# Moving small tiles in SBUF so that moving operands and weights lie a multiple of 256 bytes apart, in a two-layer trunk of SwiGLU, SSD and S5

## The chip, the cores and the metric

The kernel runs on one core of one Trainium2 chip. The metric is the device time of one execution in microseconds (us); times below one microsecond are in nanoseconds (ns). Times come from timed runs and from one execution recorded by the hardware profiler.

## The reference

The input is `x` of 512 tokens by 1024 channels in float32. Two layers follow each other, and each is a half-weighted SwiGLU, a token mixer, and another half-weighted SwiGLU. The mixer of the first layer is a Mamba-2 SSD, that of the second an S5 diagonal state space model.

```python
def swiglu(h, w_in, w_out):                      # w_in 1024 x 5632, w_out 2816 x 1024
    gate, up = jnp.split(h @ w_in, 2, axis=-1)
    return (jax.nn.silu(gate) * up) @ w_out

for i in range(2):
    x = x + 0.5 * swiglu(rmsnorm(x, ffn1_norm[i]), ffn1_w_in[i], ffn1_w_out[i])
    h = rmsnorm(x, mix_norm[i])
    x = x + (ssd_mixer(h, ...) if i == 0 else s5_mixer(h, ...))
    x = x + 0.5 * swiglu(rmsnorm(x, ffn2_norm[i]), ffn2_w_in[i], ffn2_w_out[i])
return rmsnorm(x, final_norm)
```

The SSD mixer projects to 6176 columns, convolves over time, scans in chunks over 32 heads with a state of 128, gates, normalises and projects 2048 channels back to 1024. The S5 mixer scans 64 groups of 16 channels with a complex state of 64, applies a GELU and a gated projection of 1024 to 2 x 1024.

## The kernel before

Activations lie transposed: channels on the 128 partitions, 512 tokens along the free dimension. `xT` is the residual stream, eight tiles of 128 x 512. Matrix products keep nearly all of float32's precision: each operand is split into a high part, rounded to TensorE's faster float32 format, and the low rest, and three products are added into one PSUM bank. `proj` does this for one output tile of 128 channels, over `n` slices of 128 input channels:

```python
for k in range(n):
    PE.matmul(ps, hi[:, k], H[k], start=first and k == 0, stop=False)             # L276
    PE.matmul(ps, hi[:, k], L[k], start=False, stop=False)                        # L277
    PE.matmul(ps, lo[:, k], H[k], start=False, stop=last and k == n - 1)          # L278
```

The second argument is the weights (128 x 128, 512 bytes of a partition), the third the moving operand (128 x 512, 2048 bytes of a partition). Weights arrive by DMA in `wst`; ScalarE rounds them into `whi` (L267), VectorE writes the rest into `wlo` (L269). The moving operands have names by stage:

- `hH`, `hL`: the normalised input of an FFN or of the SSD mixer (pool `hpool`). In the S5 mixer the same tiles hold some of its gate weights.
- `ah`, `al`: the product of gate and up inside an FFN, moving operand of its out projection (pool `ffn`, on the right side of SBUF).
- `yh`, `yl`: the SSD mixer's output, moving operand of its out projection (pool `ssd`).
- `gh`, `gl`: the S5 mixer's GELU output, moving operand of its gated projection (pool `s5`).
- `hx`, `hy`: sums for the second layer's in projections, which use a Winograd form with seven products of 256 columns in place of eight (`Seven`, L361). Two of its weight tiles, `wh22` and `wl22`, come from the pool `ffn`. `Seven.prod` adds one of the seven products:

```python
for j in range(KD // 2):
    bh, bl = self.pr.B[bn, j]
    for w_, b_ in ((hi, bh), (hi, bl), (lo, bh)):
        PE.matmul(ps, w_[:, j], b_, start=nm not in self.open, stop=False, skip_group_check=True)   # L361
```

An FFN's hidden width of 2816 is worked in three parts of 8, 7 and 7 slices of 128. For each part all in projections of the part run first (moving operand `hH`, `hL`), then eight out projections, one for each of the eight `xT` tiles (moving operand `ah`, `al`), so a stretch of in projections and a stretch of 8 x 3 x 7 = 168 or 8 x 3 x 8 = 192 matmuls of out projections take turns:

```python
pd = mm_ps()
proj(pd, load_w(w_out[a * 128:b * 128, d * 128:(d + 1) * 128], b - a), AH, AL)
V.scalar_tensor_tensor(xT[d], pd, 0.5, xT[d], op0=OP.mult, op1=OP.add)      # L596
```

SBUF is handed out as two stacks. The left one grows from 16,512 bytes of each partition upward: first the pool `const`, then `wpool` (`wst`, `whi`, `wlo`), `hpool`, `work`, and above them the pools of the stages. The right one grows downward from the end and holds a filler of 24 numbers and, inside an FFN, the pool `ffn`. So whatever `const` takes moves every later tile of the left stack and none of the right one. `small` (L49 to L51) hands out small tiles, padded to 32 numbers, that is 128 bytes. In `const`, `small` makes `kmask` and `qres` (L71, L72, selection masks for the S5 mixer), `cols0` to `cols3` (L96, columns of gains and biases, read by `col`) and `warm` (L106, one column used only at the start). In the SSD mixer it makes `acol`, `cse`, `dce` and the two `raw` tiles, which lie below `yh` and `yl` in their stack.

The order of work is written out by hand for TensorE (`manual_schedule`); for the other engines a scheduler sets it when the program is built. Weights are loaded by SP's queue ahead of use, through four `wst`, three `whi` and three `wlo` buffers.

Of the kernel before, what the change touches and what calls it, by code (L numbers as in the profile page):

```python
# [9 lines left out]
F32 = mybir.dt.float32  # L10
# [21 lines left out]
def trunk_kernel(ctx, tc, x, ffn1_norm, ffn1_w_in, ffn1_w_out, mix_norm, ffn2_norm, ffn2_w_in, ffn2_w_out,  # L32
# [4 lines left out]
    V, S, G, PE = nc.vector, nc.scalar, nc.gpsimd, nc.tensor  # L37

    const = ctx.enter_context(tc.tile_pool(name="const", bufs=1))
    const.tile([128, 64], F32, name="fill_left")  # L40
    right = ctx.enter_context(tc.tile_pool(name="right", bufs=1, side="right"))
    right.tile([128, 24], F32, name="fill_right")
    wpool = ctx.enter_context(tc.tile_pool(name="wpool", bufs=3))
# [4 lines left out]

    def small(pool, p, n, name, **kw):  # L49

        return pool.tile([p, -(-n // 32) * 32], F32, name=name, **kw)[:, :n]  # L51

    def mm_ps():
        return psum.tile([128, 512], F32, tag="mm", name="mm", bufs=4)
# [1 line left out]
    def aux_ps():  # L56
        return psum.tile([128, 512], F32, tag="aux", name="aux", bufs=4)
# [5 lines left out]
    def rows_ap(src, r0, n, w=128):  # L63
        return bass.AP(tensor=src.tensor, offset=src.offset + r0 * w, ap=[[w, n], [1, w]])
# [3 lines left out]
    make_identity(nc, ident)  # L68
    ones = const.tile([128, 128], F32, name="ones")
    V.memset(ones, 1.0)  # L70
    kmask = small(const, 128, 16, "kmask")  # L71
    qres = small(const, 128, 8, "qres")  # L72
    qsel = const.tile([128, 128], F32, name="qsel")

    def masks():
# [17 lines left out]


    vrow = [xin.tile([n, 128], F32, name=f"vrow{i}") for i, n in enumerate((104, 128, 18, 16))]
    cols = [small(const, 128, v.shape[0], f"cols{i}") for i, v in enumerate(vrow)]  # L96
    C = {"f1": (3, 0), "cw": (1, 0), "sd": (2, 0), "dtb": (2, 16), "al": (2, 17)}

    def cols_of(i):
# [3 lines left out]
        V.tensor_copy(cols[i], p[:, :n])  # L103

    tc.keep_in_program_order(nc.scalar.dma_start(vrow[3], rows_ap(ffn1_norm, 0, 16)))
    warm = small(const, 128, 1, "warm")  # L106
    r = 0
    for nm, src, n in (("mix", mix_norm, 16), ("f2", ffn2_norm, 16), ("fin", final_norm, 8),
                       ("gn", ssd_gate_norm, 16), ("cb", ssd_conv_b, 32), ("gb", s5_glu_b, 16)):
# [1367 lines left out]
    with tc.manual_schedule(engines={mybir.EngineType.Activation, mybir.EngineType.DVE, mybir.EngineType.PE}):  # L1477
# [23 lines left out]
        p = aux_ps()  # L1501
# [114 lines left out]
```

## Time and profile before

| | |
|---|---|
| median of three timed runs | 2073.85 us (2071.47 to 2077.07) |
| profiled execution, its own time | 2071.94 us |
| profiled execution, span from first to last instruction | 2070.2 us |
| mean granted TensorE clock | 0.989 of full speed |
| TensorE busy | 2028.3 us, 98% of the span |
| VectorE, ScalarE, GpSimd busy | 1410.9, 849.9 and 95.2 us |
| matmuls of the split format with 512 columns | 7128 |
| matmuls of the split format with 256 columns | 2016 |

In rows of the profile PE is a matmul on TensorE and PEld a weight load, which runs beside the matmuls; DVE is VectorE, ACT ScalarE, POOL GpSimd, SP SyncE. `mm<-hH,whi` reads: writes the PSUM tile `mm` from the moving tile `hH` and the weights `whi`. A group's row ends with the count, the busy time in us with the mean in ns, and the idle time ahead of it with what ended it. A row of the timeline begins with start and duration in us. The row of an operation's durations has its least, its median and its greatest in ns.

### The profile page before, as it was taken

The numbers are of one execution on the slowest core, as the hardware profiler recorded it, in microseconds if no ns is written. First come the engines' busy times: TensorE is split into PE (matmuls) and PEld (weight loads), VectorE is DVE, ScalarE is ACT, GpSimd is POOL, SyncE is SP. The second block draws the span as 40 slices with busy tenths as digits, with TensorE's granted clock in tenths as the row PEclk, the third lists the DMA queues.
The fourth block names the chain that finished last, engine by engine and source line by source line (L and its number), as shares of the span: only waits on it lengthen the run. The fifth ranks groups of instructions, "written<-read, shape, count | busy, mean of one in ns | idle before, by whom it ended". The sixth has DMA issues, their size and how long they took to land.

```text
span 2070.2 us, 29322 instructions
## 1 busy us (share of the span) xinstructions
PE 2028.3 (98%) x11555; PEld 1704.8 (82%) x11555; DVE 1410.9 (68%) x2390; ACT 849.9 (41%) x1394; POOL 95.2 (5%) x148
## 2 busy tenths in 40 slices
PE   9999999999999999999999999999996999999997
PEld 7888888888878887877778888898885889888896
DVE  6889445688875887568854776574768577556574
ACT  5223233556653564333422443242454444233343
POOL 1000000021110110000000000000011000000000
PEclk9999999999999999999999999999997999999999
DMA  6354542343333324435553223323387123333341
GB/s 183 99 157 160 150 112 84 109 123 99 120 118 92 105 74 147 131 117 157 151 160 96 88 82 113 92 80 107 108 277 244 51 70 114 102 92 94 91 119 55
DMA packets 411529, 244.42 MB, mean 118 GB/s; under 512 B 44952, under 2 KB 396864, under 8 KB 411136
## 3 DMA queue, kind: packets, MB, share of 16 engines
q1 hardware_dynamic: 381968, 203.19, 34.1%
q0 software_dynamic: 7984, 25.46, 3.7%
q10 hardware_dynamic: 21440, 13.91, 2.2%
q8 instruction: 90, 1.47, 0.3%
q14 instruction: 47, 0.39, 0.1%
HBM read 217.74 MB, written 24.25 MB: 117 GB/s over the span
## 4 chain that ended last, share of the span: by engine, by line
PE 91%; DVE 5%; ACT 2%; issue 1%; DMA 0%; SPq 0%; DVEq 0%; ACTq 0%
PE mm L276 25%; PE mm L277 25%; PE mm L278 25%; PE mm L361 12%; PE aux L836 1%; DVE cv L697 1%; DVE wlo L269 0%; PE aux L778 0%; PE aux L1349 0%; PE aux L741 0%; PE aux L829 0%; DVE z L1331 0%; PE aux L278 0%; PE aux L277 0%; PE aux L276 0%
## 5 line engine op out<-in xcount | busy, mean ns | idle before, releaser
L276 PE MATMUL mm<-hH,whi 128*128 128x512 f32 x1416 | 558.1, 394 | 0.6 <-DVE gt L570 0.6
L277 PE MATMUL mm<-hL,whi 128*128 128x512 f32 x1416 | 553.4, 391 | 0.0
L278 PE MATMUL mm<-hH,wlo 128*128 128x512 f32 x1416 | 552.8, 390 | 0.0
L267 ACT CAST whi<-wst 128x1024 fp32r<-128x1024 f32 (+2 forms) x269 | 267.6, 998 | 585.9 <-PE mm L277 443.8
L269 DVE TENSOR_TENSOR wlo<-wst,whi 128x1024 fp32r<-128x1024 f32 (+2 forms) x269 | 310.6, 1157 | 34.6 <-ACT whi L267 32.3
L278 PEld LDWEIGHTS mm<-hH,wlo 128*128 128x128 f32 x1416 | 266.0, 188 | 57.2 <-DVE wlo L269 0.6
L276 PEld LDWEIGHTS mm<-hH,whi 128*128 128x128 f32 x1416 | 266.2, 188 | 56.6 <-issue 2.7
L277 PEld LDWEIGHTS mm<-hL,whi 128*128 128x128 f32 x1416 | 266.3, 188 | 53.0 <-issue 0.6
L277 PE MATMUL mm<-al,whi 128*128 128x512 f32 x704 | 278.3, 395 | 0.0
L278 PE MATMUL mm<-ah,wlo 128*128 128x512 f32 x704 | 278.2, 396 | 0.0
L276 PE MATMUL mm<-ah,whi 128*128 128x512 f32 x704 | 277.8, 396 | 0.0
L596 DVE SCALAR_TENSOR_TENSOR xT<-mm,xT 128x512 f32<-128x512 f32 x96 | 66.0, 689 | 161.1 <-PE mm L278 160.8
L277 PEld LDWEIGHTS mm<-al,whi 128*128 128x128 f32 x704 | 132.4, 188 | 31.4 <-issue 0.6
L278 PEld LDWEIGHTS mm<-ah,wlo 128*128 128x128 f32 x704 | 132.4, 188 | 31.3 <-issue 0.2
L276 PEld LDWEIGHTS mm<-ah,whi 128*128 128x128 f32 x704 | 132.4, 188 | 31.0 <-issue 0.4
L305 DVE TENSOR_TENSOR wlo<-wst,whi 128x1024 fp32r<-128x1024 f32 x88 | 107.6, 1223 | 26.3 <-ACT whi L300 26.3
L300 ACT CAST whi<-wst 128x512 fp32r<-128x512 f32 x176 | 100.3, 621 | 21.8 <-PE mm L277 18.1
L573 DVE TENSOR_TENSOR up<-mm,rbc 128x512 f32<-128x512 f32 x44 | 30.3, 689 | 83.8 <-PE mm L278 83.5
L697 DVE SCALAR_TENSOR_TENSOR cv<-raw,cols,cv 128x512 f32<-128x512 f32 x96 | 81.0, 850 | 7.6 <-ACT cv L695 6.7
L361 PE MATMUL mm<-hH,whi 128*128 128x256 f32 x288 | 82.5, 286 | 0.3 <-ACT up L378 0.2
L361 PE MATMUL mm<-hH,wlo 128*128 128x256 f32 x288 | 82.0, 285 | 0.0
L361 PE MATMUL mm<-hL,whi 128*128 128x256 f32 x288 | 82.0, 285 | 0.0
(395 smaller groups left out, 2897.0 us busy)
## 6 DMA issues: line engine op xcount, KB each, us to landing
wst<-in_ffn_w_in_dram SPq DMA_DIRECT2D x176, 512.0 KB, 3.9
wst<-in_ffn_w_out_dram SPq DMA_DIRECT2D x64, 448.0 KB, 3.6
wst<-in_ssd_in_proj_dram SPq DMA_DIRECT2D x48, 512.0 KB, 3.8
wst<-in_ffn_w_out_dram SPq DMA_DIRECT2D x32, 512.0 KB, 3.6
dec<-d_cs POOLq DMA_DIRECT2D x16, 512.0 KB, 4.3
opP<-d_P SPq DMA_DIRECT2D x16, 512.0 KB, 6.5
wst<-in_s_glu_w_dram POOLq DMA_DIRECT2D x12, 512.0 KB, 5.1
d_t<-p_cs POOLq DMA_DIRECT2D x8, 512.0 KB, 4.4
```

The source lines that it names most:

```text
L267: S.copy(hi, st)
L269: V.tensor_tensor(lo, st, hi.bitcast(F32), op=OP.subtract)
L276: PE.matmul(ps, hi[:, k], H[k], start=first and k == 0, stop=False)
L277: PE.matmul(ps, hi[:, k], L[k], start=False, stop=False)
L278: PE.matmul(ps, lo[:, k], H[k], start=False, stop=last and k == n - 1)
L300: self.pin(S.copy(hi[:, hs[i]], st[i] if type(st) is list else st[:, hs[i]]))
L305: self.pin(V.tensor_tensor(lo[:, b], a, hi[:, b].bitcast(F32), op=OP.subtract))
L361: PE.matmul(ps, w_[:, j], b_, start=nm not in self.open, stop=False, skip_group_check=True)
L573: V.tensor_tensor(up, pu, pr.rbc, op=OP.mult)
L596: V.scalar_tensor_tensor(xT[d], pd, 0.5, xT[d], op0=OP.mult, op1=OP.add)
L697: V.scalar_tensor_tensor(cv, raw[:, 1 + j:T + 1 + j], col("cw", j * 32 + ct), cv, op0=OP.mult, op1=OP.add)
L836: PE.matmul(py[hh * 64:(hh + 1) * 64, s], st["dtx"][:, c, k0:k0 + 64], M[:, hh, s], start=True, stop=True)
```

## The change

A filler at the bottom of `const` goes, `small` pads to 64 numbers (256 bytes) in place of 32, and five small tiles of `const` (`kmask`, `qres`, `cols2`, `cols3`, `warm`) become slices of one tile `few` of 64 numbers.

```diff
     const = ctx.enter_context(tc.tile_pool(name="const", bufs=1))
-    const.tile([128, 64], F32, name="fill_left")
...
     def small(pool, p, n, name, **kw):
-        return pool.tile([p, -(-n // 32) * 32], F32, name=name, **kw)[:, :n]
+        return pool.tile([p, -(-n // 64) * 64], F32, name=name, **kw)[:, :n]
...
-    kmask = small(const, 128, 16, "kmask")
-    qres = small(const, 128, 8, "qres")
+    few = const.tile([128, 64], F32, name="few")
+    kmask = few[:, 0:16]
+    qres = few[:, 16:24]
...
-    cols = [small(const, 128, v.shape[0], f"cols{i}") for i, v in enumerate(vrow)]
+    cols = [small(const, 128, v.shape[0], f"cols{i}") for i, v in enumerate(vrow[:2])] + [few[:, 26:44], few[:, 44:60]]
...
-    warm = small(const, 128, 1, "warm")
+    warm = few[:, 24:25]
```

In both programs each engine's instructions stand in the same order and with the same shapes; after the change ScalarE has one more wait on semaphores, for DMAs of GpSimd's queue in the first FFN. The starts of the tiles move: `const` shrinks by 640 bytes (256 + 5 x 128 go, 256 come), and everything above it on the left stack sinks by as much, but for `yh` and `yl`, below which five small tiles of the SSD mixer grow by 128 bytes each. This is where the tiles of the wide matmuls begin in a partition, by the places that the two programs give them (a tile with several buffers by its first; its other buffers are multiples of 512 bytes further):

| tile | start before | modulo 256 | start after | modulo 256 |
|---|---|---|---|---|
| `whi`, `wlo` (weights) | 53,248 and 65,536 | 0 | 52,608 and 64,896 | 128 |
| `hH`, `hL` | 77,824 and 94,208 | 0 | 77,184 and 93,568 | 128 |
| `hy`, `hx` | 121,344 and 129,536 | 0 | 120,704 and 128,896 | 128 |
| `gh`, `gl` | 193,536 and 209,920 | 0 | 192,896 and 209,280 | 128 |
| `yh`, `yl` | 188,032 and 204,416 | 128 | 188,032 and 204,416 | 128 |
| `ah`, `al` | 196,480 and 212,864 | 128 | 196,480 and 212,864 | 128 |
| `wh22`, `wl22` (weights) | 188,288 and 190,336 | 128 | 188,288 and 190,336 | 128 |

Slices of these tiles begin at further multiples of 512 bytes, so the last columns hold for every wide matmul. Before, 2496 matmuls of 512 columns (those of `ah`, `al`, `yh`, `yl`) and 288 of 256 columns (those of `wh22`, `wl22`) have a moving operand 128 bytes off a multiple of 256 from their weights; after, none has. Tiles that other engines use moved too: `wst` begins at 36,864 (0 modulo 256) before and at 36,224 (128) after, the sums in `rbc` and `sq` likewise from 0 to 128, while `xT`, `cv` and `y` are at 128 before and after.

## The prediction, made before the changed kernel ran

> **What bounds the kernel now.** I read the page's busy times first, then the chain that ended last, then the groups of instructions.
>
> ```profile
> span 2070.2 us, 29322 instructions
> PE 2028.3 (98%) x11555; PEld 1704.8 (82%) x11555; DVE 1410.9 (68%) x2390; ACT 849.9 (41%) x1394; POOL 95.2 (5%) x148
> PE 91%; DVE 5%; ACT 2%; issue 1%; DMA 0%; SPq 0%; DVEq 0%; ACTq 0%
> L276 PE MATMUL mm<-hH,whi 128*128 128x512 f32 x1416 | 558.1, 394 | 0.6 <-DVE gt L570 0.6
> L277 PE MATMUL mm<-hL,whi 128*128 128x512 f32 x1416 | 553.4, 391 | 0.0
> L278 PE MATMUL mm<-hH,wlo 128*128 128x512 f32 x1416 | 552.8, 390 | 0.0
> L277 PE MATMUL mm<-al,whi 128*128 128x512 f32 x704 | 278.3, 395 | 0.0
> L278 PE MATMUL mm<-ah,wlo 128*128 128x512 f32 x704 | 278.2, 396 | 0.0
> L276 PE MATMUL mm<-ah,whi 128*128 128x512 f32 x704 | 277.8, 396 | 0.0
> L276 PE MATMUL mm<-yh,whi 128*128 128x512 f32 x128 | 51.9, 405 | 0.3 <-ACT yh L855 0.3
> ```
>
> TensorE is the bound: 98% of the span, 91% of the chain, and almost no idle time ahead of any wide group. So what one matmul costs is what counts. The last column but one is the duration of a record, whose end is modelled and which overlaps the next; it hints at a few ns between hH and ah, but it isn't a price. The price is the distance from one start to the next, so I took stretches of the timeline in which nothing else runs on TensorE. Each pair below is the first and the last matmul of a stretch without a break.
>
> ```profile
> 265.80 0.39 PE L276 MATMUL mm<-hH,whi 128*128 128x512 f32 x1
> 341.75 0.39 PE L278 MATMUL mm<-hH,wlo 128*128 128x512 f32 x1
> ...
> 341.97 0.40 PE L276 MATMUL mm<-ah,whi 128*128 128x512 f32 x1
> 380.94 0.39 PE L278 MATMUL mm<-ah,wlo 128*128 128x512 f32 x1
> ...
> 1405.68 0.39 PE L276 MATMUL mm<-ah,whi 128*128 128x512 f32 x1
> 1440.30 0.40 PE L278 MATMUL mm<-ah,wlo 128*128 128x512 f32 x1
> ...
> 788.71 0.48 PE L276 MATMUL mm<-yh,whi 128*128 128x512 f32 x1
> 813.66 0.39 PE L278 MATMUL mm<-yh,wlo 128*128 128x512 f32 x1
> ...
> 1625.81 0.48 PE L276 MATMUL aux<-gh,whi 128*128 128x512 f32 x1
> 1696.18 0.39 PE L277 MATMUL mm<-gl,whi 128*128 128x512 f32 x1
> ...
> 38.24 0.50 PE L276 MATMUL mm<-hH,whi 128*128 128x512 f32 x1 [0.64 <-DVE gt L570]
> 103.42 0.39 PE L278 MATMUL mm<-hH,wlo 128*128 128x512 f32 x1
> ```
>
> The stretches hold 336, 168, 150, 108, 311 and 288 matmuls. From start to start that is 75.95/335 = 226.7 ns for hH, 38.97/167 = 233.4 and 34.62/149 = 232.3 ns for ah and al, 24.95/107 = 233.2 for yh and yl, 70.37/310 = 227.0 for gh and gl, and 65.18/287 = 227.1 for hH in a stretch with some restarts. The clock is not the difference:
>
> ```profile
> 265.80:341.80 76.00, 76.00 (x337) 62.93 (x336) 33.95 (x43) 24.77 (x30) 0.00 (x0) 1.00 0.36 101
> 342.00:380.90 38.90, 38.90 (x168) 31.32 (x167) 24.49 (x32) 16.64 (x23) 2.54 (x3) 1.00 0.33 88
> 1626.00:1696.00 70.00, 70.00 (x311) 57.93 (x310) 47.14 (x68) 31.94 (x53) 6.17 (x7) 1.00 0.23 68
> ```
>
> Each row is a stretch, with busy time of PE, PEld, DVE, ACT and POOL, the granted clock (1.00 in all), and the share and rate of the DMAs. Put beside the starts of the tiles in the table above, the wide matmuls fall into two kinds. Moving tile a multiple of 256 bytes from the weights: about 227 ns. Moving tile 128 bytes off: about 233 ns. The gh stretch is the control. Its tiles lie as high in SBUF as ah and yh (193,536 bytes and up, against 196,480 and 188,032), it streams its weights through the same copies, VectorE is busier there (47.14 of 70 us, 67%, against 24.49 of 38.90, 63%), and it runs at 227.0. So neither place nor the load on other engines makes the 233.
>
> **The change part by part.** The order of instructions on each engine is the same before and after, and no DMA changes queue; what moves is addresses alone. ScalarE gets one semaphore wait more, in the first FFN; waits of that kind cost 38 ns at the median by the row below, on an engine that is 41% busy, so I cost it at nothing.
>
> ```profile
> L267 ACTq EVENT_SEMAPHORE  x243: 17/38/8805, 24.3 to 2035.8; - x122
>   PE mm L277: 443.8, 140
>   DMA wst<-in_ffn_w_out_dram: 2.2, 1
> ```
>
> *The ah, al, yh and yl matmuls.* There are 3 x 704 + 3 x 128 = 2496 of them, all 128 bytes off before and all aligned after. Before, I take 232.85 ns, half way between the two long ah stretches (233.4 and 232.3); yh's 233.2 lies between them. After, I take 227.1, from the hH stretch with restarts, since these groups are cut by other work too; a stretch without restarts (226.7) would be too kind. The gain is 2496 x 5.75 ns = 14.4 us. The bounds: 2496 x (233.4 - 226.7) = 16.7 us above; below, 128 bytes costs nothing after all and the gain is zero.
>
> *Aligned stretches that come right after a misaligned one.* The hH matmuls after an interruption start a few ns slow and settle within about ten:
>
> ```profile
> 1592.48 0.50 PE L276 MATMUL mm<-gh,hH 128*128 128x512 f32 x1
> 1592.82 0.40 PE L277 MATMUL mm<-gl,hH 128*128 128x512 f32 x1
> 1594.90 0.39 PE L277 MATMUL mm<-gl,hH 128*128 128x512 f32 x1
> ```
>
> From 1592.82 to 1594.90 stand nine steps of 231 ns, at aligned addresses. So 227 is a rhythm that a stream falls into, and the misaligned streams are those that never do. A handful of hH stretches follow ah directly; ten matmuls x 4 ns x some eight places is 0.3 us, which I leave out.
>
> *The 288 products with wh22 and wl22* (256 columns) are also 128 bytes off before. Their rows:
>
> ```profile
> 1363.42 0.41 PE L361 MATMUL mm<-hx,wh 128*128 128x256 f32 x2
> 1364.87 0.40 PE L276 MATMUL mm<-hH,whi 128*128 128x512 f32 x1
> ...
> 1372.38 0.28 PE L361 MATMUL mm<-hH,wlo 128*128 128x256 f32 x1
> 1373.10 0.28 PE L361 MATMUL mm<-hH,wlo 128*128 128x256 f32 x1
> ```
>
> Twelve of them take 1.45 us, 120.8 ns each; the aligned ones beside them take 0.72/6 = 120.0. The gain is 288 x 0.8 ns = 0.2 us; I take 0.2. Here the weights are the ones moved by 128 and the moving tile stands at 0, and it costs next to nothing. I note that against my own reading.
>
> *The other 6360 wide matmuls* (4632 of 512 columns, 1728 of 256) stay aligned to their weights, but both operands move from a multiple of 256 bytes to 128 past one. No wide matmul of the trace has both operands there, so no row prices it. Bounds: 0 if only the distance counts, and the loss of the second rival if the tile's own place counts. I take 0, since the gh row shows that a stream's rhythm survives moves of 100 kB as long as the distance is kept.
>
> *Weight DMAs and copies* now write tiles that start 128 bytes further. The row of ScalarE's waits above says what hides this: of the time ahead of its 269 weight copies, 443.8 us ended with TensorE freeing a buffer, and 2.2 us, once, with a weight transfer. A transfer longer by a few tenths costs nothing there. VectorE works on tiles at 128 bytes today (xT, cv, y) and has a third of the span idle.
>
> *Given back.* TensorE faster by 2.5% in the out projections asks the weight copies to come faster by 2.5%; in the ah stretch ScalarE is busy 16.64 and VectorE 24.49 of 38.90 us, so they can. Only near the hand-overs between stages, where TensorE waits on others anyway (DVE is 5% of the chain), is time lost again: 5% of 14.4, or 0.7 us.
>
> Sum: -14.4 - 0.2 + 0.7 = -13.9 us. The profiled execution took 2071.9 us by its own time, so it would take 2058.0. It lies 1.9 us below the median of the three timed runs (2073.85), and those spread over 5.6 us. I put the new median at 2059, between 2058.0 and 2059.9.
>
> **The rivals.** *The distance does nothing.* The two operands don't meet, and ah and yh are slow for a reason that I have not seen; the wh22 rows (120.8 against 120.0) speak for it, the gh stretch against. The time stays at 2072 to 2074. The Trainium skill's page "TensorE: Matmul & The Clock Gate" says this in effect: under "Step-by-step: what each phase is for", TensorE has two independent SBUF read ports, one for the moving operand and one for the weights, and under "Back-to-back issue gap" a warm matmul of 512 columns takes 512/2.4 + 2.5 = 216 ns, with no address in it. By that page the change moves nothing. The trace doesn't agree with its figure: 226.7 at best, and 233 beside it, at a full clock.
>
> *The moving tile's own place counts.* All moving tiles of the 227 ns stretches start at a multiple of 256 bytes, all of the 233 ns ones at 128 past it, and weights at 128 hardly cost anything (wh22): the trace is just as well explained by the moving tile alone, whatever the weights do. Then the change spoils everything else: ah and yh stay as they are, 4632 matmuls of 512 columns go from 227.1 to 232.85, +26.6 us, and 1728 of 256 columns lose up to 0.8 ns, +1.4 us, together 2100 us. What decides is whether both operands at 128 are as good as both at 0. For distance speaks that wh22 does change the rhythm though its moving tile stands at 0 (steps that vary, 120.8 on average, instead of an even 120.0); a rule on the moving tile alone has no reason for that.
>
> *Partial.* The pattern might repeat at 512 bytes rather than 256. After the change ah lies at a multiple of 512 from its weights and yh 256 off. Then yh's 384 matmuls gain nothing, 2.2 us less: 2061.
>
> **How the numbers follow.** Distance counts, in full or in part: 0.76, at 2059, its own range 2054.5 (16.7 us off the profiled run) to 2064. Nothing happens: 0.11. The moving tile's own place: 0.13. To leave out no more than two in ten, the range must reach into the second case: 2054 to 2073. A measurement here tells about 0.3% (6 us) from no change; -14 us is -0.7%. So faster 0.76, same 0.11, slower 0.13.
>
> **What would show it.** The ah stretch of the first layer's FFNs must step by 226.7 to 227.1 ns, and the three ah groups fall to a mean of 389 to 391 ns like gh's; the yh groups too. The hH groups must stay at 390 to 394. If hH rises to 395 or more while ah stays, the second rival holds; if both stay, the first. If ah steps by 227 and the span doesn't follow, waits on VectorE's and ScalarE's weight copies must have grown in the out projections, which would break my step on what is given back.

## The result, and the profile after

The changed kernel took 2061.3 us (median of four runs, 2058.3 to 2062.1), the kernel before on the same chip 2074.0 us. The ratio is 0.9936, with a 95% interval of 0.9918 to 0.9953. Five further rounds in a later session gave 0.9936 again (0.9922 to 0.9950). The profiled execution took 2058.3 us, 13.6 us less than the one before (2071.9).

From the page of the changed kernel, the span, the busy times, and the groups that answer to those of before:

```profile
span 2056.6 us, 29323 instructions
PE 2013.2 (98%) x11555; PEld 1703.2 (83%) x11555; DVE 1410.3 (69%) x2390; ACT 850.5 (41%) x1394; POOL 93.6 (5%) x148
L276 PE MATMUL mm<-hH,whi 128*128 128x512 f32 x1416 | 558.1, 394 | 0.6 <-DVE gt L570 0.6
L277 PE MATMUL mm<-hL,whi 128*128 128x512 f32 x1416 | 552.7, 390 | 0.0
L278 PE MATMUL mm<-hH,wlo 128*128 128x512 f32 x1416 | 552.5, 390 | 0.5 <-DVE wlo L269 0.5
L277 PE MATMUL mm<-al,whi 128*128 128x512 f32 x704 | 274.5, 390 | 0.0
L278 PE MATMUL mm<-ah,wlo 128*128 128x512 f32 x704 | 274.3, 390 | 0.0
L276 PE MATMUL mm<-ah,whi 128*128 128x512 f32 x704 | 274.1, 390 | 0.0
L276 PE MATMUL mm<-yh,whi 128*128 128x512 f32 x128 | 51.4, 401 | 0.4 <-ACT yh L855 0.4
```

The mean duration of the ah and al groups fell from 395 and 396 ns to 390, one above the 389 where gh's stood before and stand now; hH and hL moved by 1 ns at most. TensorE is still busy for 98% of the span, and the other engines did the same work. The steps from start to start show it more sharply. The timeline of the changed kernel, first and last matmul of stretches that correspond to those of before:

```profile
263.42 0.39 PE L276 MATMUL mm<-hH,whi 128*128 128x512 f32 x1
339.35 0.39 PE L278 MATMUL mm<-hH,wlo 128*128 128x512 f32 x1
339.58 0.39 PE L276 MATMUL mm<-ah,whi 128*128 128x512 f32 x1
377.43 0.39 PE L278 MATMUL mm<-ah,wlo 128*128 128x512 f32 x1
...
784.32 0.47 PE L276 MATMUL mm<-yh,whi 128*128 128x512 f32 x1
808.70 0.39 PE L278 MATMUL mm<-yh,wlo 128*128 128x512 f32 x1
```

The first two rows hold 336 matmuls in 75.93 us, 226.7 ns a step as before. The next two hold the same 168 matmuls that took 38.97 us; they now take 37.85, 226.6 ns a step in place of 233.4. The last two hold 108 matmuls, 227.9 ns a step in place of 233.2. The granted clock is the one before the last two numbers of each row here, and it is 1.00 in the hH and ah stretches, as it was before:

```profile
263.30:339.30 76.00, 76.00 (x337) 62.94 (x336) 33.95 (x43) 24.82 (x30) 0.00 (x0) 1.00 0.38 102
339.50:377.40 37.90, 37.90 (x169) 31.38 (x168) 24.48 (x32) 16.65 (x23) 2.33 (x3) 1.00 0.33 89
```

Both programs have the same 11,555 matmul records in the same order, so every step can be compared with its own step before. Summed by moving tile, the changes are: ah and al -12.3 us (2112 matmuls), yh and yl -1.6 us (384), the products with wh22 and wl22 -0.3 us, hy +0.8 us, no other wide family (hL is next, with -0.3) more than 0.3 us either way; all together -13.8 us.

### The profile page after: what moved, and what is told of

Same layout as the page of the kernel before. It is cut to its first block, busy times and chain, and to the rows that moved or that the text cites. A ratio compares the mean times of both kernels' runs of the same rounds, so it can differ in the third digit from the quotient of the medians.

```text
span 2056.6 us, 29323 instructions
## 1 busy us (share of the span) xinstructions
PE 2013.2 (98%) x11555; PEld 1703.2 (83%) x11555; DVE 1410.3 (69%) x2390; ACT 850.5 (41%) x1394; POOL 93.6 (5%) x148
## 4 chain that ended last, share of the span: by engine, by line
PE 88%; DVE 6%; ACT 2%; DMA 2%; issue 1%; SPq 0%; ACTq 0%; DVEq 0%
PE mm L276 24%; PE mm L277 24%; PE mm L278 24%; PE mm L361 11%; DMA wst<-in_s_glu_w_dram 1%; DVE wlo L269 1%; PE aux L836 1%; DVE cv L697 1%; PE aux L778 0%; DMA d_u<-s5u 0%; DMA wst<-in_ffn_w_in_dram 0%; PE aux L1349 0%; PE aux L741 0%; PE aux L829 0%; DVE z L1331 0%
## 5 line engine op out<-in xcount | busy, mean ns | idle before, releaser
L276 PE MATMUL mm<-hH,whi 128*128 128x512 f32 x1416 | 558.1, 394 | 0.6 <-DVE gt L570 0.6
L278 PE MATMUL mm<-hH,wlo 128*128 128x512 f32 x1416 | 552.5, 390 | 0.5 <-DVE wlo L269 0.5
L278 PEld LDWEIGHTS mm<-hH,wlo 128*128 128x128 f32 x1416 | 266.0, 188 | 57.6 <-DVE wlo L269 0.9
L276 PEld LDWEIGHTS mm<-hH,whi 128*128 128x128 f32 x1416 | 266.2, 188 | 56.5 <-issue 2.6
L278 PE MATMUL mm<-ah,wlo 128*128 128x512 f32 x704 | 274.3, 390 | 0.0
L276 PE MATMUL mm<-ah,whi 128*128 128x512 f32 x704 | 274.1, 390 | 0.0
L276 PEld LDWEIGHTS mm<-ah,whi 128*128 128x128 f32 x704 | 132.2, 188 | 27.5 <-issue 0.4
L278 PEld LDWEIGHTS mm<-ah,wlo 128*128 128x128 f32 x704 | 132.2, 188 | 27.5 <-issue 0.2
```

## The experiments

All start from the changed kernel and only move tiles, by fillers. In the traces TensorE and VectorE execute the same operations in the same order as in the changed kernel, but for one to three pairs of small ones (on opP and p_cs) that change places in some runs. "Step" is the distance from one start to the next, as above. A family is "off" when its distance from its weights isn't a multiple of 256 bytes, and a distance is meant modulo 256 bytes.

**One distance spoilt again.**

```diff
-    right.tile([128, 24], F32, name="fill_right")
+    right.tile([128, 56], F32, name="fill_right")
```

> The changed kernel with one edit: the filler on the right stack grows by 32 numbers, so that ah and al (and the weight tiles wh22, wl22) start at 0 modulo 256 while the other weights and all moving tiles of the left stack stay at 128. Theory (only the distance of moving tile and weights modulo 256 counts): ah and al step by 232.9 ns again as before the change, hH, gh and yh stay at 227 to 228, the products with wh22 go from 119.4 to about 120.4; 2112 x 5.8 ns = 12.3 us, so 2073 to 2074 us and a ratio to the kernel before of about 1.000. Rival (the gain came from something else that the change moved, such as the weights' own place or the tiles of the other engines): ah stays at 227.1 and the time at 2061 us, ratio 0.994.

Measured: 2072.9 us, ratio 0.9991 (0.9982 to 1.0001). Its timeline, for 192 matmuls of the second layer:

```profile
1280.06 0.40 PE L276 MATMUL mm<-ah,whi 128*128 128x512 f32 x1
1324.63 0.39 PE L278 MATMUL mm<-ah,wlo 128*128 128x512 f32 x1
```

44.57/191 = 233.4 ns: ah is as slow as before the change, though it now starts at 0 modulo 256 and the weights at 128, the reverse of before. yh and hH both kept 227.6 ns on average (all their steps below 260 ns). So 128 bytes on the right stack take nearly all of the gain away; what is left fits yh's 1.6 us, and the other moves of the change carry nothing that shows. The rival is out.

**Every operand at 0 in place of 128.**

```diff
+    const.tile([128, 32], F32, name="fill_left")
...
-    right.tile([128, 24], F32, name="fill_right")
+    right.tile([128, 56], F32, name="fill_right")
```

> The changed kernel with the left stack raised by 128 bytes and the right one lowered by 128: every distance is a multiple of 256 as in the changed kernel, but all operands of wide matmuls start at 0 modulo 256 in place of 128. ah, yh and the products with wh22 now lie 256 past a multiple of 512 from their weights. Theory (distance modulo 256): all streams step by 227 to 228 ns, 2061 us, ratio 0.994. Rival (place): starting at 0 differs from starting at 128 for some stream, by 2 ns a matmul or more, 10 us or more over all. Rival (the pattern repeats at 512 only): ah rises from 227.1 towards 233, 2073 us.

Measured: 2060.4 us, ratio 0.9928 (0.9913 to 0.9942), not to be told from the changed kernel's. The 192 matmuls of ah that run from

```profile
1275.37 0.39 PE L277 MATMUL mm<-ah,whi 128*128 128x512 f32 x1
1318.66 0.39 PE L279 MATMUL mm<-ah,wlo 128*128 128x512 f32 x1
```

step by 43.29/191 = 226.6 ns (line numbers are one higher in this kernel). For these streams place doesn't count, distance does; and since ah lies here an odd multiple of 256 bytes from its weights, the pattern repeats at 256 bytes, not only at 512.

**The largest family put off by 128 bytes.**

```diff
     wpool = ctx.enter_context(tc.tile_pool(name="wpool", bufs=3))
+    ctx.enter_context(tc.tile_pool(name="hpad", bufs=1)).tile([128, 32], F32, name="fill_h")
     hpool = ctx.enter_context(tc.tile_pool(name="hpool", bufs=8))
+    ctx.enter_context(tc.tile_pool(name="wpad", bufs=1)).tile([128, 32], F32, name="fill_w")
```

> The changed kernel with 128 bytes of filler ahead of the pool of hH and hL and 128 behind it: hH and hL start at 0 modulo 256, all weights and other moving tiles at 128. Theory (distance): the 4248 matmuls of 512 columns on hH and hL go from 227.4 to 232.9 ns, +23 us, the 864 of 256 columns lose 0.5 ns each, ah, yh and gh stay; 2085 us, ratio 1.005. The glu matmuls whose weights lie in the hH tiles (96 of 512 columns) go to 233 as well. Rival (only tiles high in SBUF, where ah and yh lie, feel it): hH stays at 227.4, 2061 us, ratio 0.994.

Measured: 2083.0 us, ratio 1.0043 (1.0026 to 1.0060). In its timeline hH is the slow stream and ah the fast one (L278 to L280 are L276 to L278 of the changed kernel, here and in the runs with other distances):

```profile
267.11 0.40 PE L278 MATMUL mm<-hH,whi 128*128 128x512 f32 x1
345.27 0.39 PE L280 MATMUL mm<-hH,wlo 128*128 128x512 f32 x1
...
105.46 0.39 PE L278 MATMUL mm<-ah,whi 128*128 128x512 f32 x1
148.78 0.39 PE L280 MATMUL mm<-ah,wlo 128*128 128x512 f32 x1
```

78.16/335 = 233.3 ns against 43.32/191 = 226.8. The price belongs to the distance, not to a tile or to a side of SBUF. Against the 2060.4 of the run before, from the same session, it is +22.6 us for 4248 matmuls on hH and hL and 96 with weights in the hH tiles, 5.2 ns each; 23 us had been expected.

**Half of the weights put off.** The pool of `wlo` is taken out of `wpool` and set 128 bytes further.

```diff
+    ctx.enter_context(tc.tile_pool(name="lpad", bufs=1)).tile([128, 32], F32, name="fill_l")
+    lpool = ctx.enter_context(tc.tile_pool(name="lpool", bufs=3))
+    ctx.enter_context(tc.tile_pool(name="lpad2", bufs=1)).tile([128, 32], F32, name="fill_l2")
...
-        lo = wpool.tile([128, KD, 128], F32R, name="wlo", bufs=3)[:, :kt]
+        lo = lpool.tile([128, KD, 128], F32R, name="wlo", bufs=3)[:, :kt]
```

> The changed kernel with wlo in a pool of its own, 128 bytes further: only the low half of the weights is off by 128 from the moving tiles. In each triple the second matmul (L277) has aligned weights of its own but the weights loaded beside it, those of the third, are off; the third (L278) has weights of its own that are off while aligned ones are loaded beside it. Theory next (a stream collides with the load of the next weights): L277 steps longer than L276 and L278. Theory own (it is the matmul's own weights): L278 steps longer. Either way a step of the triple is 227 plus about a third of 6 ns, 229 on average, so 7128 x 2 ns = +14 us, 2075 us. If rhythm matters more than the single collision, all three lines step unevenly and the mean may come nearer to 233, +40 us.

Measured: 2088.9 us (one run), +27.6 us on the changed kernel: twice the 14 us of the first two theories, and below the 40 of the third. Two triples of its timeline (a triple is the three matmuls of one k; L279 to L281 are L276 to L278 of the changed kernel):

```profile
1299.68 0.39 PE L279 MATMUL mm<-ah,whi 128*128 128x512 f32 x1
1299.91 0.40 PE L280 MATMUL mm<-al,whi 128*128 128x512 f32 x1
1300.14 0.40 PE L281 MATMUL mm<-ah,wlo 128*128 128x512 f32 x1
1300.37 0.39 PE L279 MATMUL mm<-ah,whi 128*128 128x512 f32 x1
1300.60 0.40 PE L280 MATMUL mm<-al,whi 128*128 128x512 f32 x1
1300.83 0.40 PE L281 MATMUL mm<-ah,wlo 128*128 128x512 f32 x1
1301.07 0.39 PE L279 MATMUL mm<-ah,whi 128*128 128x512 f32 x1
```

Two triples take 1.39 us, 231.7 ns a step (231.1 over a stretch of 192). Over the whole run the median steps are 227 after the first of a triple, 232 after the second, 234 after the third. A weight load starts 3 or 4 ns after the matmul ahead of its own (nearly all records of the changed kernel), so it runs beside that one. Neither theory holds alone: the matmul beside which the displaced weights are loaded is slower, and so is the one that uses them while aligned weights are loaded. That the moving read and the weight read get in each other's way is a reading that fits, but no row shows it: the traces hold starts and durations, not reads. Why both steps are longer stays open.

**Other distances.** Fillers as above, of other sizes.

> The changed kernel with fillers that set other distances from the weights: hH and hL 32 bytes (modulo 256), ah and al 64, and gh, yh, hx and hy 96. At 0 all of them step by 227, at 128 by 232.9. Theory even (the two 128-byte halves of a 256-byte pattern collide in proportion to the overlap): the loss grows with the distance up to 128, so hH about 228.5, ah 230, gh and yh 231.5 ns. Theory any (every distance but 0 breaks the rhythm): all three families step by about 233 ns, 4632 more matmuls than before, about 2100 us. Theory hole (some distance lets the moving stream and the weight load pass each other): one of the three falls below 227, down to 216 ns at best, the step of the float32 products wx by btok.

> The same with hH and hL 160 bytes from the weights (modulo 256), ah and al 192, and gh, yh, hx and hy 224. Theory even: the loss shrinks again towards 256, so hH about 231.5, ah 230, gh and yh 228.5 ns. Theory any: all about 233 ns. Theory hole: one of the three below 227. If the sign of the distance matters (the load trails the moving stream by 3 ns), the values differ from those at 96, 64 and 32 by a ns or more.

Measured: 2090.9 and 2101.8 us, one run each. First and last matmul of stretches of 336 (hH), 192 (ah) and 311 (gh), for the run with 32, 64 and 96 bytes, and for hH of the run with 160, 192 and 224:

```profile
269.38 0.40 PE L278 MATMUL mm<-hH,whi 128*128 128x512 f32 x1
347.54 0.40 PE L280 MATMUL mm<-hH,wlo 128*128 128x512 f32 x1
...
106.86 0.40 PE L278 MATMUL mm<-ah,whi 128*128 128x512 f32 x1
150.58 0.39 PE L280 MATMUL mm<-ah,wlo 128*128 128x512 f32 x1
...
1641.88 0.48 PE L278 MATMUL aux<-gh,whi 128*128 128x512 f32 x1
1714.23 0.39 PE L279 MATMUL mm<-gl,whi 128*128 128x512 f32 x1
```

```profile
272.21 0.39 PE L278 MATMUL mm<-hH,whi 128*128 128x512 f32 x1
350.69 0.39 PE L280 MATMUL mm<-hH,wlo 128*128 128x512 f32 x1
```

That is 233.3 ns at 32 bytes (hH), 228.9 at 64 (ah), 233.4 at 96 (gh) and 234.3 at 160 (hH); the other two families of the second run gave 233.3 at 192 (ah) and at 224 (gh). Nearest is the theory that every distance but 0 breaks the rhythm, with one exception at 64. No distance falls below 226.7, so the theory of a hole is out; 32 and 160 were tried on hH alone. A further run asked whether the value at 64 belonged to ah:

> The changed kernel with hH and hL 64 bytes from the weights (modulo 256), ah and al 64 as well but another multiple of 256 further than in the run with 32, 64 and 96, and gh, yh, hx and hy 192. Theory (the step depends on the distance modulo 256, whatever the tile): hH steps by 229.1 as ah did at 64, ah again by 229.1, gh and yh by 233.3 as ah did at 192. Rival (the value at 64 belonged to ah or to the right side): hH at 64 steps by about 233.

Measured: 2072.9 us, one run.

```profile
267.21 0.40 PE L278 MATMUL mm<-hH,whi 128*128 128x512 f32 x1
343.89 0.39 PE L280 MATMUL mm<-hH,wlo 128*128 128x512 f32 x1
```

76.68/335 = 228.9 ns: hH steps at 64 as ah did. ah, at 64 plus another 256, gave 228.9 in its stretch too, and gh at 192 gave 233.5, as ah had. The 96 products of the S5 mixer whose weights lie in the hH tiles say the same with other weights: their own distance is 64 in the runs with 32 and with 160 bytes, where the last twelve steps of each stretch average 228.8 to 228.9 ns, and 128 in the run with hH put off and in this one, where they average 231.6 to 233.4; in the changed kernel, at 0, it is 226.7. In all these runs the step of a 512-column stream goes by the distance modulo 256, whatever the tile. It does so to about 1 ns: of the ten long ah stretches of the kernel before, all at 128, six settle at 233.3 and four at 232.3 to 232.4.

**A better distance for 256 columns.** In the same runs some 256-column products went the other way: their steps fell from 120.0 ns at 0 to 117 and 118 at 32 (wh22 and wl22; hH and hL) and to 115.7 on average at 192 (hx). At 96 they kept 119.8 (hx). Two last kernels use this for `hx` and `hy`, which are read with 256 columns alone (here the second, with 192 bytes; the first has 8 and 56 numbers), timed against the changed kernel once more.

```diff
+    ctx.enter_context(tc.tile_pool(name="xpad", bufs=1)).tile([128, 48], F32, name="fill_x")
     hx.append(ctx.enter_context(tc.tile_pool(name="hx", bufs=6, reuse_waits="tile")))
+    ctx.enter_context(tc.tile_pool(name="xpad2", bufs=1)).tile([128, 16], F32, name="fill_x2")
```

> The changed kernel as it is, timed once more in five rounds for a narrower interval and as the base of the next run. From the distances: 2496 x 5.8 ns = 14 us off the kernel before, a ratio of 0.9935 within 0.001.

> The changed kernel with 32 bytes of filler ahead of the pool of hx and hy and 224 behind it: these tiles, moving operands of 256 columns alone, lie 32 bytes past a multiple of 256 from their weights, wh22 and wl22 with them; everything else keeps its distance of 0. Theory (at 256 columns the best distance is 32, where wh22 stepped by 117.0 and hL by 117.0 ns against 120.0 at 0): 864 products on whi and wlo go from 119.9 to 117, 288 on wh22 and wl22 from 119.4 to 117, together 3.2 us off, 2058 us and a ratio of about 0.992. Rival (the first 512-column matmuls behind these products lose the rhythm and give it back): no difference from the changed kernel, 2061 us.

> The same as the run with hx and hy at 32 bytes, with 192 bytes of filler ahead and 64 behind: hx and hy lie 192 bytes from all their weights, the distance at which they stepped by 115.7 and 115.5 ns when hH was at 64; everything else keeps 0. Theory (distance, by width): 864 products go from 119.9 to about 115.7 and 288 on wh22 and wl22 from 119.4 to about 116, together 4.6 us off the changed kernel, 2057 us, ratio about 0.991, 512-column matmuls unchanged at 227 to 228. Rival (given back behind them, or 115.7 belonged to the other fillers of that run): hx stays near 118 to 120 or hH loses as much, 2059 to 2061 us.

| kernel | median us | ratio to before | 95% interval |
|---|---|---|---|
| changed kernel, again | 2061.4 | 0.9936 | 0.9922 to 0.9950 |
| hx, hy at 32 bytes | 2058.6 | 0.9924 | 0.9912 to 0.9937 |
| hx, hy at 192 bytes | 2055.5 | 0.9912 | 0.9895 to 0.9929 |

Each ratio is to the kernel before, run on the same chip in the same session; the last row is from a session of its own.

A stretch of 36 products on hx, first in the changed kernel, then with hx at 192:

```profile
1215.94 0.28 PE L361 MATMUL mm<-hx,whi 128*128 128x256 f32 x1
1220.14 0.28 PE L361 MATMUL mm<-hx,wlo 128*128 128x256 f32 x1
```

```profile
1216.92 0.29 PE L361 MATMUL mm<-hx,whi 128*128 128x256 f32 x1
1220.91 0.28 PE L361 MATMUL mm<-hx,wlo 128*128 128x256 f32 x1
```

4.20/35 = 120.0 ns against 3.99/35 = 114.0, less than the 115.7 that had been expected; wh22 came to 117.8 rather than 116. With hx at 32 the same products came to 117.9, where 117 had been expected. With hx at 192, hH kept 227.3 ns on average, so nothing was given back behind the products. 864 x 6 ns is 5.2 us, and the median is 5.9 us below the changed kernel's, from another session. The intervals overlap, so the times alone are not proof of the gain; the steps are what shows it. This is the fastest of the kernels tried.

The 115.7 was a mean of two values. In the run with hH at 64, hx lies by its fillers at the same addresses as in the last kernel, 192 from its weights, and two stretches of 36 products that follow each other are these:

```profile
1227.15 0.28 PE L363 MATMUL mm<-hx,whi 128*128 128x256 f32 x1
1231.27 0.28 PE L363 MATMUL mm<-hx,wlo 128*128 128x256 f32 x1
...
1248.06 0.28 PE L363 MATMUL mm<-hx,whi 128*128 128x256 f32 x1
1252.03 0.28 PE L363 MATMUL mm<-hx,wlo 128*128 128x256 f32 x1
```

4.12/35 = 117.7 ns against 3.97/35 = 113.4. Of the 22 such stretches eleven run at the one step and eleven at the other; in the last kernel all 22 run at 113.9. So at 256 columns the distance alone doesn't set the step. What chooses between the two wasn't tried; the products ahead of these, on hH, lie at 64 in the one run and at 0 in the other.

## Why the prediction held, step by step

**The main term.** It was 2496 x 5.75 ns = 14.4 us; the steps show 12.3 + 1.6 = 13.9. Of ah and al it was right (12.1 forecast). Of yh and yl it was about a third too large, 2.2 us against 1.6. Their eleven stretches are short, 12 to 108 matmuls, cut by the scan's own matmuls. The price of 233.2 read from the longest one holds a first step of 318 ns that the change doesn't touch (314 after); without it that stretch ran at 232.4 before and runs at 227.1 now. Behind such a cut the next nine steps are slow at either distance (231 ns on average after the change), so short stretches gain less. (The rows that the prediction shows for such a start, from 1592.48 on, are of gh with weights in the hH tiles, not of hH as a moving tile.)

**wh22.** Forecast 0.2 us, measured 0.3. The doubt noted there, that weights off by 128 cost next to nothing, came from looking at 256 columns only: at 512 columns displaced weights cost as much as a displaced moving tile (weights at 128 and hH at 0 in the third experiment, 233.3 ns).

**The other 6360 wide matmuls.** Taken at 0; the largest changes are hy's +0.8 us, which is a wait (below), and hL's -0.3 us. The gain of hH stretches right behind ah, left out at 0.3 us, is 0.1 us or less: ten places, -0.03 us over the first twelve steps of each, all together. The rival that the moving tile's own place counts would have shown hH at 395 ns and more; it stayed at 390 to 394, and with all operands at 0 nothing changed either.

**The rival that nothing happens** is out: with TensorE's operations in the same order the same stream steps by 226.7 or by 233.3 ns as its distance from the weights is 0 or 128. Beside it stood the rule of the Trainium skill's page "TensorE: Matmul & The Clock Gate", section "Step-by-step: what each phase is for", of two independent read ports. The measurements decide against what was drawn from it, that the change moves nothing; they don't show the ports. The prediction also set the 216 ns of the Trainium skill's page "TensorE: Matmul & The Clock Gate", section "Back-to-back issue gap", against the trace; that section gives it for a matmul by itself and not for a stream that loads weights for each, as all streams here do. No run here shows such a matmul, so that comparison decided nothing.

**The partial rival**, a pattern of 512 bytes, is out as well: yh lies an odd multiple of 256 from its weights in the changed kernel and settles at 226.7 ns, and so does ah with all operands at 0.

**Given back.** Forecast 0.7 us for time lost again at the hand-overs between stages; hy's +0.8 us is such a place. Among the waits of TensorE in the changed kernel that the list of before has not is this one:

```profile
PE mm L361 <- DVE hy L231: 0.4, 1, 0.4
```

TensorE reaches the second layer's products sooner and waits for VectorE's low half of hy; the two steps there grew by 0.66 us. That it came out near the 0.7 us is luck: the forecast took DVE's 5% of the chain as a share of the gain, and no row had priced this place. Weight copies of the out projections didn't become a bound, as had been argued: the ah groups have no idle time ahead of them.

**The sum and the median.** -13.9 us was forecast, -13.8 came: the mechanism was right, but the agreement to 0.1 us is partly luck. yh's gain fell 0.6 us short, and hL's -0.3 and smaller changes made most of that up. For the median 2059 was forecast and 2061.3 measured; the profiled run lies 3.0 us below its median where the one before lay 2.0 below. The lower end that the prediction gave to its main case, 2054.5, doesn't follow from its working: 2071.9 - 16.7 is 2055.2.

## What to carry to other kernels

Where TensorE is the bound, read the distance from start to start, not the duration, and compare streams of one shape with each other: two steady values for one shape are a question worth asking. Before trusting an address as the cause, look for a stream that shares everything else (here gh) and then move one filler. And the best distance has to be measured for each width: of those tried here, 0 was best for 512 columns and 192 for 256, where the same distance also gave two different steps.

## What the runs showed of the hardware

- The step of a 512-column matmul beside a 128-column weight load depends on the distance of the two operands modulo 256 bytes: 226.7 ns at 0, 228.9 at 64, 232.3 to 234.3 at 32, 96, 128, 160, 192 and 224 (long stretches; granted clock 1.00).
- At 256 columns the order is another: on hx 120.0 ns at 0, 117.9 at 32, 114.0 at 192 when only hx and hy are moved. The distance alone doesn't set it: at 192 with hH at 64, stretches ran at 117.7 or at 113.4. Why the two widths disagree, and why 64 costs a third of what 128 does, stays open.
- A stream at distance 0 settles into an even step of 226 to 227 ns within about ten matmuls after an interruption. At 128 the stretches looked at never do: in the first experiment, with ah put off again, its steps alternate between 229 and 237 or 238 ns from the third step of a stretch of 192 matmuls to the last.
